# Value projection of a decoder layer: where the second value weights are split and where the second tokens are transposed

## The chip, the cores and the metric

One core of a Trainium2 chip runs the whole layer. The metric is the device time of one execution in microseconds (us). The kernel before took 1835.76 us, the median of three runs (1833.45 to 1837.6).

## What is computed

One layer over 1024 tokens of width 1024, in float32: a half-step SwiGLU network, a token mixer and a second half-step SwiGLU, each followed by a residual sum and a LayerNorm. The part around the change is the input of the token mixer:

```python
x = layer_norm(ALPHA * x + (1 + g1) * (MACARON * y), ln1_g[l], ln1_b[l])
h = modulate(x, sh2, sc2)
y = token_mix(h, w_in[l], b_forget[l], swa_sinks[l], grp_gain[l], w_out[l])
...
proj = h @ w_in
q_a, k_a, v_a, q_b, k_b, v_b, f_logit = jnp.split(proj, idx, axis=-1)
o_a = swa_sink_attention(q_a, k_a, v_a, swa_sinks)
log_f = jax.nn.log_sigmoid(f_logit.astype(jnp.float32) + b_forget.astype(jnp.float32))
o_b = forgetting_attention(q_b, k_b, v_b, log_f)
```

The value projection is the part of `h @ w_in` that gives v_b, v_a and the eight forget logits: 512 + 128 + 8 columns.

## The kernel before, in words

**Precision.** Each float32 operand of a product is held as a high part, rounded to the matrix engine's fp32r format, and a low part, the rest. `split` (lines 101 to 103) makes them: ACT copies the high part (L102), DVE subtracts it (L103). A product is three matmuls, `mm3` (lines 105 to 108: L106, L107, L108).

**Stages.** The first SwiGLU ends with `down` (line 365), which works the tokens in two halves of 512: `xa` are the first tokens, `xb` the second, four tiles of 128 tokens by 1024 each. Its last step multiplies by the gate and subtracts into the tiles of `xb` (L490, L491). The first tokens are normalised and transposed while the second are still being multiplied, with the helper `ln_steps` (line 680). It returns twelve steps: four normalisations of one token tile each, and eight chunks.

- A normalisation (`ln_norm`, line 168) is on DVE two statistics instructions (L158, L159), their merge (L161), an addition (L163), then a power on POOL (L165), then one pass over the tile on DVE (L170).
- A chunk (`ht_chunk`, line 181) transposes one 128-column slice of the four token tiles on PE into a PSUM bank "tp" (L185, four matmuls with the identity), and ACT writes it out with the modulation (L186). `h2_split` (line 699) splits it: the high part on DVE for even chunks (L707), on ACT for odd ones (L705), the low part on DVE (L708).

**The value projection** (lines 733 to 771) multiplies the transposed, modulated tokens by two weights: `wv1`, 320 columns, and `wv2`, 328 columns. `wv_load` brings each in eight slices of 128 rows: one load into a tile of ring "u" (L739, queued on SP), ACT's high copy (L740), DVE's low part (L741). The kernel before calls it for both weights, then runs the four normalisations of the second tokens, then calls `rows2` (line 145), which loads two rows of LayerNorm weights over all partitions (L150) and scales them on ACT (L152).

Then come sixteen projections. The outer loop runs over the halves of the tokens, the next over the two weights, the inner over four token tiles; each projection is eight products, 24 matmuls, into a PSUM bank "mm". ACT copies its high part out (L761), DVE its low part (L762), SP stores both (L763); with the second weight DVE also adds the forget bias (L765). In the first half a projection is followed by at most two of the eight chunks of the second tokens: chunk 1 after projection 2, and so on, chunks 7 and 8 after projection 8. In the second half each is followed by `park_zn` (line 676): an affine of one token tile on DVE (L673, L674) and its store (L678).

After the stage come the projections of queries and keys (`proj`, line 813; their weights are loaded at L528), and then the attention, in which further projections are mixed in.

**What sets the order.** Loads and stores are queued on SP. Buffers are rings: "u" has 6 tiles, "h" 14, "b" 2, "z" and "q" 4 each, "t" 7, "w" 6; PSUM has 3 banks "mm", 2 "tp", 2 "y", 1 "o". A tile is given out again when its last reader is done. The order in which each engine runs its instructions is fixed when the kernel is built, from the program text and from when their operands and buffers are expected.

Of the kernel before, what the change touches and what calls it, by code (L numbers as in the profile page):

```python
# [30 lines left out]
NV1 = 5 * HD  # L31
NV2 = 5 * HD + NH
# [14 lines left out]
def layer_kernel(ctx, tc, xT, x, c, adaT, adab, wg1, wu1, wd1, wqk, wv1, wv2, bf, sinks,  # L47
# [16 lines left out]
    def st(tag, shape, dt=F32):  # L64
        assert 4 * math.prod(shape[1:]) <= RING[tag][1], (tag, shape)
        return mk(sb, shape, dt, tag, RING[tag][0])
# [7 lines left out]
    def psum(tag):  # L74
        return mk(ps, [P, HT], F32, tag, BANK[tag])
# [29 lines left out]
    def mm3(o, lh, ll, rh, rl, start, stop):  # L105
        T.matmul(o, lh, rh, start=start, stop=False)  # L106
        T.matmul(o, lh, rl, start=False, stop=False)  # L107
        T.matmul(o, ll, rh, start=False, stop=stop)  # L108
# [36 lines left out]
    def rows2(i, scale=None, ring="h"):  # L145

        rr = [st("b", [P, D]) for _ in range(2)] if ring == "b" else [st("h", [P, 2, D])]
        rr = rr if ring == "b" else [rr[0][:, q] for q in range(2)]
        for q in range(2):
            DMA.dma_start(rr[q], lnrow[i + q].partition_broadcast(P))  # L150
            if scale is not None:
                A.mul(rr[q], rr[q], scale)  # L152
        return rr
# [510 lines left out]
    def tok(t):  # L664
        return slice(t * P, (t + 1) * P)
# [10 lines left out]
    def park_zn(zt, hf, k, rows, park):  # L676
        affine(zt[k], rows)
        DMA.dma_start(park[tok(hf * 4 + k), :], zt[k])  # L678

    def ln_steps(zt, hf, m, dst, split_to, park=None):  # L680

        def norm(k):
            ln_norm(zt[k])
            if park is not None:
                DMA.dma_start(park[tok(hf * 4 + k), :], zt[k])

        def chunk(d):
            t = dst(d)
            ht_chunk(zt, m, d, t)
            split_to(d, t)  # L690
        return [lambda k=k: norm(k) for k in range(4)] + [lambda d=d: chunk(d) for d in range(KD)]

    def run_all(steps):
        for s in steps:
            s()
# [3 lines left out]
    def h2_split(hf):  # L699
        def f(d, t):  # L700
            if d % 4 == 0:
                h2[hf].append(htiles())
            hi, lo = h2[hf][d // 4]
            if d % 2:
                A.copy(hi[:, d % 4], t)  # L705
            else:
                V.tensor_copy(hi[:, d % 4], t)  # L707
            V.tensor_tensor(lo[:, d % 4], t, hi[:, d % 4].bitcast(F32), ALU.subtract)  # L708
        return f

    def h2c(hf, d):
        hi, lo = h2[hf][d // 4]
        return hi[:, d % 4], lo[:, d % 4]
# [17 lines left out]
    fz = const([P, NT, NH], "fz")  # L731

    def wv_load(src, ncol):
        r = []
        for d0, nk in ((0, 3), (3, 3), (6, 2)):
            w = st("h", [P, 2, nk, ncol], F32R)
            for k in range(nk):
                s = st("u", [P, ncol])
                DMA.dma_start(s, src[:, d0 + k, :])  # L739
                A.copy(w[:, 0, k], s)  # L740
                V.tensor_tensor(w[:, 1, k], s, w[:, 0, k].bitcast(F32), ALU.subtract)  # L741
                r.append((w[:, 0, k], w[:, 1, k]))
        return r

    wva = wv_load(wv1, NV1)
    wvb = wv_load(wv2, NV2)
    steps = ln_steps(xb, 1, mod2, t_tile, h2_split(1))
    run_all(steps[:4])
    r1 = rows2(0, ALPHA, "b")
    for hf in range(2):  # L750
        for pz, (w, ncol) in enumerate(((wva, NV1), (wvb, NV2))):
            for k in range(4):
                t = hf * 4 + k
                p = psum("mm")
                for d in range(KD):
                    hi, lo = h2c(hf, d)
                    mm3(p[:, :ncol], hi[:, k * P:(k + 1) * P], lo[:, k * P:(k + 1) * P],
                        w[d][0], w[d][1], d == 0, d == KD - 1)
                vs = st("w", [P, 5, P], F32R)
                pv = p[:, :5 * HD].rearrange("p (h c) -> p h c", h=5)  # L760
                A.copy(vs[:, :, :HD], pv)  # L761
                V.tensor_tensor(vs[:, :, HD:], pv, vs[:, :, :HD].bitcast(F32), ALU.subtract)  # L762
                DMA.dma_start(vd[pz * 5:pz * 5 + 5, tok(t), :].rearrange("h t c -> t h c"), vs.bitcast(F32))  # L763
                if pz:
                    V.tensor_tensor(fz[:, t], p[:, 5 * HD:NV2], bfb, ALU.add)  # L765
                if hf == 0:
                    if t or pz:
                        steps[3 + t + 4 * pz]()
                    if t == 3 and pz:
                        steps[11]()  # L770
                else:
                    park_zn((xa, xb)[pz], pz, k, r1, xpark[0])

# [432 lines left out]
    def h3_dst(hf):  # L1206
        def f(d):
            if hf == 0:
                hd.append(st("z" if d < 4 else "q", [P, S]))
            return halves(hd[d])[hf]  # L1210
        return f

    def h3_split(hf):
        def f(d, t):
            n = "B%d%d" % (d // 4 + 1, hf + 1)
            if n[2] == "2":
                return
            if d % 4 == 0:
                ops2[n] = htiles()
            split(ops2[n][0][:, d % 4], ops2[n][1][:, d % 4], t)  # L1220
        return f
# [16 lines left out]
    steps = ln_steps(z2[4:], 1, mod3, h3_dst(1), h3_split(1), xpark[1])  # L1238
# [150 lines left out]
```

## Time and profile before

| | |
|---|---|
| median of three runs | 1835.76 us (1833.45 to 1837.6) |
| the profiled execution | 1834.09 us |
| its span, from the first to the last instruction | 1832.1 us |
| mean granted clock of TensorE | 0.985 |
| busy: PE, DVE, ACT | 96%, 84%, 42% of the span |
| sixteen projections of the stage | 661.2 to 731 us |

Shares of the span say which engine is the limit on the whole, not in a stage. In a line of the trace, L12 is line 12 of the kernel; out<-in names the rings, so that `mm<-h,h` at 128x320 or 128x328 is a matmul of the value projection with the first or the second weights. The bracket behind a line tells how long the engine stood idle before it and which instruction ended that. Matmuls overlap, so the distance from one start to the next says more than the duration of one.

### The profile page before, as it was taken

Reading aid. Unit: us, or ns where it says so; the run is one execution under the profiler, and the core shown is the slowest. Engines: PE = TensorE matmul, PEld = TensorE weight load, DVE = VectorE, ACT = ScalarE, POOL = GpSimd, SP = SyncE. Lnnn points to the kernel's source line nnn. Section 1 sums busy time; section 2 is a strip of 40 time slices with the busy share of each in tenths; the row PEclk is TensorE's granted clock in tenths of the full one; section 3 lists DMA queues with packets and bytes.
Section 4 is the critical chain, followed back from the end, with each engine's and each line's share of the span. In section 5 each row is a group of like instructions: output and inputs, shape, how many; then the busy total and the mean of one; then the engine's idle time right before and its main releaser. Section 6 shows DMA issues by size and latency. Waiting matters only on the chain.

```text
span 1832.1 us, 23557 instructions
## 1 busy us (share of the span) xinstructions
PE 1755.3 (96%) x8114; PEld 1444.7 (79%) x8114; DVE 1546.1 (84%) x2805; ACT 764.7 (42%) x1465; POOL 23.0 (1%) x32
## 2 busy tenths in 40 slices
PE   7999999999999989999889899999999999999995
PEld 5788888888888879877667777778888888888884
DVE  7999999999597995378678797899788887878999
ACT  5432333233544442277356461543233333344480
POOL 0000000000000000000000000000000000000000
PEclk9999999999999999999989999999999999999998
DMA  9355555558754245855958863333223232675442
GB/s 360 127 197 178 193 193 193 170 173 290 233 167 143 86 134 180 242 148 154 229 143 198 215 205 107 138 109 128 97 99 131 88 108 92 223 231 166 133 144 80
DMA packets 163175, 303.44 MB, mean 166 GB/s; under 512 B 15384, under 2 KB 47728, under 8 KB 163056
## 3 DMA queue, kind: packets, MB, share of 16 engines
q1 hardware_dynamic: 163056, 301.94, 52.1%
q8 instruction: 64, 1.05, 0.2%
q14 instruction: 55, 0.45, 0.1%
HBM read 224.17 MB, written 77.71 MB: 165 GB/s over the span
## 4 chain that ended last, share of the span: by engine, by line
PE 73%; DVE 15%; DMA 6%; ACT 3%; issue 2%; SPq 0%; POOL 0%; DVEq 0%; ACTq 0%; POOLq 0%
PE y L106 10%; PE y L107 10%; PE y L108 10%; PE mm L106 9%; PE mm L108 9%; PE mm L107 9%; PE o L106 3%; PE o L108 3%; PE o L107 3%; DVE w L103 2%; DVE h L103 2%; DMA q<-cum_d 2%; PE tp L107 1%; PE tp L108 1%; PE tp L1114 1%
## 5 line engine op out<-in xcount | busy, mean ns | idle before, releaser
L102 ACT CAST w<-u 128x512 fp32r<-128x512 f32 x303 | 186.6, 622 | 393.1 <-PE y L108 160.2
L106 PE MATMUL y<-h,w 128*128 128x512 f32 x728 | 287.7, 395 | 5.0 <-ACT h L102 2.1
L107 PE MATMUL y<-h,w 128*128 128x512 f32 x728 | 285.6, 392 | 0.0
L108 PE MATMUL y<-h,w 128*128 128x512 f32 x728 | 285.2, 392 | 0.0
L103 DVE TENSOR_TENSOR w<-u,w 128x512 fp32r<-128x512 f32 x303 | 206.5, 686 | 23.4 <-ACT w L102 22.1
L106 PE MATMUL mm<-h,w 128*128 128x512 f32 x528 | 207.7, 394 | 18.7 <-ACT h L102 15.6
L107 PE MATMUL mm<-h,w 128*128 128x512 f32 x528 | 206.7, 392 | 0.3 <-DVE h L103 0.2
L108 PE MATMUL mm<-h,w 128*128 128x512 f32 x528 | 206.7, 392 | 0.0
L106 PEld LDWEIGHTS y<-h,w 128*128 128x128 f32 x728 | 137.5, 189 | 33.5 <-ACT h L102 2.5
L108 PEld LDWEIGHTS y<-h,w 128*128 128x128 f32 x728 | 137.0, 188 | 26.6
L107 PEld LDWEIGHTS y<-h,w 128*128 128x128 f32 x728 | 137.0, 188 | 26.3
L102 ACT CAST w<-t 128x512 fp32r<-128x512 f32 x106 | 65.5, 621 | 185.1 <-PE mm L108 70.3
L106 PEld LDWEIGHTS mm<-h,w 128*128 128x128 f32 x528 | 100.2, 190 | 40.9 <-ACT h L102 16.0
L107 PEld LDWEIGHTS mm<-h,w 128*128 128x128 f32 x528 | 100.0, 189 | 22.2 <-DVE h L103 1.5
L108 PEld LDWEIGHTS mm<-h,w 128*128 128x128 f32 x528 | 99.9, 189 | 21.3 <-DVE w L103 1.0
L102 ACT CAST z<-u 128x512 fp32r<-128x512 f32 x88 | 54.8, 623 | 105.2 <-PE y L108 46.8
L103 DVE TENSOR_TENSOR z<-u,z 128x512 fp32r<-128x512 f32 x88 | 60.5, 689 | 35.7 <-ACT z L102 35.6
L103 DVE TENSOR_TENSOR t<-tp,t 128x512 fp32r<-128x512 f32 (+1 forms) x126 | 72.8, 586 | 18.4 <-ACT t L102 17.7
L102 ACT CAST t<-tp 128x512 fp32r<-128x512 f32 (+1 forms) x126 | 61.8, 502 | 48.3 <-PE tp L1114 47.4
L102 ACT CAST w<-h 128x512 fp32r<-128x512 f32 x111 | 68.2, 617 | 29.4 <-PE o L108 10.5
L103 DVE TENSOR_TENSOR w<-h,w 128x512 fp32r<-128x512 f32 x111 | 75.6, 686 | 1.8 <-ACT w L102 1.8
L103 DVE TENSOR_TENSOR w<-t,w 128x512 fp32r<-128x512 f32 x106 | 72.8, 689 | 1.4 <-ACT w L102 0.8
(356 smaller groups left out, 3948.1 us busy)
## 6 DMA issues: line engine op xcount, KB each, us to landing
u<-aT SPq DMA_DIRECT2D x154, 256.0 KB, 2.7
q<-in_adaT SPq DMA_DIRECT2D x56, 512.0 KB, 3.4
u<-in_wg SPq DMA_DIRECT2D x92, 256.0 KB, 3.0
u<-in_wu SPq DMA_DIRECT2D x90, 256.0 KB, 2.8
aT<-z SPq DMA_DIRECT2D x44, 512.0 KB, 3.2
h<-in_wd SPq DMA_DIRECT2D x88, 256.0 KB, 4.5
qkd<-w SPq DMA_DIRECT2D x26, 512.0 KB, 4.1
aT<-b SPq DMA_DIRECT2D x22, 512.0 KB, 4.2
```

Of the source, the lines that this page charges most:

```text
L102: A.copy(hi, src)
L103: V.tensor_tensor(lo, src, hi.bitcast(F32), ALU.subtract)
L106: T.matmul(o, lh, rh, start=start, stop=False)
L107: T.matmul(o, lh, rl, start=False, stop=False)
L108: T.matmul(o, ll, rh, start=False, stop=stop)
L1114: T.transpose(pt[:, tok(i - q0)], sps[i][:, tok(j)], ident)
```

## The change

`wv_load` no longer runs its loads and splits. It returns the list that will hold the slices and three functions, which load and split slices 1 to 3, 4 to 6, and 7 and 8. Those of the first weights are run at once. Those of the second weights are put into a list `between`, one behind each of projections 1 to 3; nothing stands behind projection 4; and the eight chunks of the second tokens stand behind projections 5 to 8, two each. The normalisations and the call of `rows2` keep their place. Nothing that is computed changes.

```diff
     def wv_load(src, ncol):
+
         r = []
-        for d0, nk in ((0, 3), (3, 3), (6, 2)):
+
+        def load(d0, nk):
             w = st("h", [P, 2, nk, ncol], F32R)
             for k in range(nk):
                 s = st("u", [P, ncol])
...
                 A.copy(w[:, 0, k], s)
                 V.tensor_tensor(w[:, 1, k], s, w[:, 0, k].bitcast(F32), ALU.subtract)
                 r.append((w[:, 0, k], w[:, 1, k]))
-        return r
-
-    wva = wv_load(wv1, NV1)
-    wvb = wv_load(wv2, NV2)
+        return r, [lambda a=a: load(*a) for a in ((0, 3), (3, 3), (6, 2))]
+
+    wva, load_a = wv_load(wv1, NV1)
+    wvb, load_b = wv_load(wv2, NV2)
+    run_all(load_a)
     steps = ln_steps(xb, 1, mod2, t_tile, h2_split(1))
     run_all(steps[:4])
+    between = [[f] for f in load_b] + [[]] + [steps[4 + 2 * k:6 + 2 * k] for k in range(4)]
     r1 = rows2(0, ALPHA, "b")
...
                 if hf == 0:
-                    if t or pz:
-                        steps[3 + t + 4 * pz]()
-                    if t == 3 and pz:
-                        steps[11]()
+                    run_all(between.pop(0))
                 else:
                     park_zn((xa, xb)[pz], pz, k, r1, xpark[0])
```

## Rows read from the trace of the kernel before

**Rows 1.** The page's parts 1 and 4: busy time, share of the span and instructions of PE; shares of the chain that ended last, by engine.

```profile
PE 1755.3 (96%) x8114; PEld 1444.7 (79%) x8114; DVE 1546.1 (84%) x2805; ACT 764.7 (42%) x1465; POOL 23.0 (1%) x32
...
PE 73%; DVE 15%; DMA 6%; ACT 3%; issue 2%; SPq 0%; POOL 0%; DVEq 0%; ACTq 0%; POOLq 0%
```

**Rows 2.** Windows of the value projection. Columns: the window in us, its length, busy us of PE, PEld, DVE, ACT and POOL, each with its count of instructions, then the granted clock of TensorE, the DMA share and GB/s.

```profile
661.20:671.50 10.30, 10.30 (x72) 10.30 (x70) 9.40 (x22) 4.72 (x10) 0.55 (x1) 1.00 0.61 179
671.50:679.00 7.50, 1.68 (x9) 0.83 (x8) 6.57 (x18) 0.79 (x2) 1.10 (x2) 0.85 0.67 217
679.00:683.50 4.50, 4.50 (x19) 4.42 (x18) 3.42 (x7) 1.43 (x2) 0.55 (x1) 0.50 0.72 218
683.50:705.00 21.50, 21.50 (x153) 21.46 (x152) 17.58 (x28) 9.20 (x16) 0.00 (x0) 1.00 0.50 175
705.00:731.00 26.00, 25.69 (x172) 25.22 (x171) 11.37 (x18) 3.26 (x8) 0.95 (x1) 1.00 0.56 190
```

**Rows 3.** PE in order of time between projections 3 and 5: start us, us from the first start to the last end, engine, line, operation, out<-in, shape, count, and in brackets the idle time before it and what ended it. Equal neighbours are merged (x4).

```profile
672.55 0.30 PE L185 MATMUL tp<-ident,z 128*128 128x128 f32 x1 [0.78 <-DVE z L170]
...
676.30 0.44 PE L185 MATMUL tp<-ident,z 128*128 128x128 f32 x2 [3.20 <-DVE z L170]
678.58 0.69 PE L185 MATMUL tp<-ident,z 128*128 128x128 f32 x2 [1.84 <-DVE z L170]
679.05 0.64 PE L106 MATMUL mm<-h,h 128*128 128x320 f32 x1
...
684.92 0.60 PE L185 MATMUL tp<-ident,z 128*128 128x128 f32 x4
685.28 0.40 PE L106 MATMUL mm<-h,h 128*128 128x328 f32 x1
```

**Rows 4.** DVE in order of time from the first statistics of the second tokens' normalisation to its last step. Columns as in the group above.

```profile
665.44 0.69 DVE L158 BATCH_NORM_STATS2 s_bn<-z 128x6 f32<-128x512 f32 x1
...
668.32 1.88 DVE L741 TENSOR_TENSOR h<-u,h 128x328 fp32r<-128x328 f32 x4 [0.90 <-ACT h L740]
670.12 0.15 DVE L163 TENSOR_SCALAR s_ve<-s_mv 128x1 f32<-128x1 f32 x1
...
670.78 0.90 DVE L741 TENSOR_TENSOR h<-u,h 128x328 fp32r<-128x328 f32 x2
671.59 0.81 DVE L170 TENSOR_SCALAR z<-z,s_mv,s_rs 128x1024 f32<-128x1024 f32 x1
672.32 0.49 DVE L741 TENSOR_TENSOR h<-u,h 128x328 fp32r<-128x328 f32 x1
673.48 0.50 DVE L741 TENSOR_TENSOR h<-u,h 128x328 fp32r<-128x328 f32 x1 [0.67 <-ACT h L740]
...
674.57 0.14 DVE L163 TENSOR_SCALAR s_ve<-s_mv 128x1 f32<-128x1 f32 x1
...
675.44 0.81 DVE L170 TENSOR_SCALAR z<-z,s_mv,s_rs 128x1024 f32<-128x1024 f32 x1
...
678.55 0.44 DVE L762 TENSOR_TENSOR w<-mm,w 128x320 fp32r<-128x320 f32 x1
...
679.78 0.81 DVE L170 TENSOR_SCALAR z<-z,s_mv,s_rs 128x1024 f32<-128x1024 f32 x1 [0.33 <-POOL s_rs L165]
```

**Rows 5.** The chain that ended last, between 661 and 684 us: start us, us, and what it was.

```profile
662.99 4.81 DMA u<-in_wv
...
669.29 3.67 DMA u<-in_wv
...
672.98 0.47 ACT h L740
```

**Rows 6.** DVE in order of time just after the normalisations. Columns as in rows 3.

```profile
680.91 1.22 DVE L673 TENSOR_TENSOR q<-q,b 128x1024 f32<-128x1024 f32 x1
682.88 0.43 DVE L707 CAST h<-t 128x512 fp32r<-128x512 f32 x1 [0.75 <-ACT t L186]
```

**Rows 7.** ACT in order of time, its copies out of PSUM of projections 1 and 3. Columns as in rows 3.

```profile
669.57 0.42 ACT L761 CAST w<-mm 128x320 fp32r<-128x320 f32 x1
...
673.35 0.42 ACT L761 CAST w<-mm 128x320 fp32r<-128x320 f32 x1
```

**Rows 8.** Windows around two gaps of PE in the attention stage. Columns as in rows 2.

```profile
880.00:883.00 3.00, 1.00 (x5) 0.79 (x5) 2.72 (x4) 0.00 (x0) 0.00 (x0) 1.00 1.10 243
1011.00:1016.00 5.00, 2.46 (x10) 1.78 (x9) 5.00 (x13) 1.40 (x5) 1.91 (x1) 0.86 1.02 311
```

**Rows 9.** SP, the engine that issues the loads and stores, in order of time. Columns as in rows 3; the us of a merged row run from the first issue to the last.

```profile
662.55 0.33 SPq L150 DMA_DIRECT2D b<-in_lnrow  x1
662.99 7.01 SPq L739 DMA_DIRECT2D u<-in_wv  x8
670.09 4.24 SPq L528 DMA_DIRECT2D u<-in_wqk  x6
```

**Rows 10.** From the view of line 739, the sixteen loads of both value weights: time from issue to landing.

```profile
DMA to landing us min/median/max: 2.1/2.3/4.3
```

**Rows 11.** Windows after the stage. Columns as in rows 2.

```profile
740.00:783.00 43.00, 43.00 (x207) 35.66 (x207) 13.13 (x33) 13.77 (x33) 0.00 (x0) 1.00 0.78 230
783.00:844.00 61.00, 60.66 (x333) 48.65 (x332) 49.30 (x139) 44.44 (x136) 0.00 (x0) 1.00 0.52 149
```

**Rows 12.** The chain that ended last, in the attention stage: start us, us, and what it was.

```profile
939.12 10.50 DMA q<-cum_d
```

## The prediction

> **What bounds the kernel now.** First the page's engine shares and its chain [rows 1]: PE is busy for 96% of the span and holds 73% of the chain that ended last; DVE comes second with 15%. Time can be won where PE stands still, and the stage to look at is the value projection. I number its projections 1 to 16, eight for the first tokens and eight for the second, each of 24 matmuls. Second, the stage's windows [rows 2]: PE is full from 661.2 to 671.5 us (72 matmuls, projections 1 to 3), works for 1.68 of the next 7.5 us, then runs 4.5 us at a granted clock of 0.50, which is the 1.2 GHz level, and is full at 1.00 from there. Third, PE's order in time [rows 3]: after projection 3 come transposes of the second tokens' first two chunks, two for each token tile, and each pair waits for that tile's normalisation (L170): 0.78, 3.20 and 1.84 us, 5.8 in all. Projection 4 starts at 679.05. It also needs one of the three PSUM banks "mm" back, and the first copy out of one on DVE (L762) starts at 678.55. So both waits are waits for DVE.
>
> Fourth, DVE's order [rows 4], which says why it is late. The normalisations begin at 665.44, but among them stand the eight splits of the second weights (L741, 128x328), and two of these wait for ACT's copy, 0.90 and 0.67 us. Fifth, the chain of waits over this stretch [rows 5]: a load of second weights of 4.81 us, later a last one of 3.67 us and its copy of 0.47, and only then the split and the normalisations of tiles two and three. A transfer that PE does not need before projection 5 holds up what it needs for projection 4.
>
> The order on an engine is not that of the program text: it takes what is ready, earlier text first. In [rows 6] an affine of the second half of the loop (L673, 680.91) runs ahead of a chunk cast of the first half (L707, 682.88) that still waited for ACT. I read the change with that rule.
>
> **The change, part by part.**
>
> The splits leave the normalisations' way. In [rows 4] they take 1.80 us (668.32 to 670.12, four), 0.81 (670.78 to 671.59, two), 0.49 and some 0.4, and the two idles add 0.90 and 0.67: 5.1 us between 665.44 and L762 at 678.55. After the change all eight stand later in the text than the normalisations. I take back 0.2 us, since the first normalisation then waits for POOL with less beside it: from the L163 at 674.57 to its L170 at 675.44 it is 0.87 us, of which one statistics instruction fills some 0.6. **4.9 us earlier** (estimate): L762 at 673.65, projection 4 at 674.15, and PE's gap from 671.6 shrinks to 2.5 us. Bounds: 0, if the list stays as it is, and 7.4 (679.05 − 671.6), if the copy out came before the normalisations; ACT's copy for it (L761) began at 669.57 [rows 7], so that is possible. I take 4.9 because it follows from the order that the rows show.
>
> The transposes move behind projections 5 to 8, two chunks, eight transposes, each. The six that ran inside PE's gap come onto the path. Four in a row from 684.92 let the next matmul start at 685.28 [rows 3], 0.09 us each: **+0.5 us**, or 0 if they still fall into what is left of the gap. The duration of one, 0.30 us at 672.55 [rows 3], is longer than this spacing, since they overlap. The Trainium skill (TensorE: Matmul & The Clock Gate, Part 4: PE-mode transpose) puts one at about 275 ns inside a kernel; the trace agrees with that as a duration, not as a spacing, and by that figure six would cost 1.65 us and the estimated saving in all would be 3.3 us instead of 4.4.
>
> The clock. It fell during the gap; the 15 matmuls and 4 transposes from 679.0 took 4.5 us at 0.50 [rows 2]. At the full clock they take 15 × 0.143 (10.30 us for 72) and 4 × 0.09, 2.5 us: the fall costs 2.0. A gap of 2.5 us remains. Elsewhere a window of 3 us with 2.0 us of gap left the clock at 1.00, and one of 5 us with 2.5 us of gap has 0.86 [rows 8]. The second is nearer: I count the fall as still there, **0 us**; if it does not come, −2.0.
>
> The second weights' loads. They keep their place on SP: the row load (L150) is already ahead of them and the projection weights (L528) behind [rows 9]. They go through a ring of six tiles "u": the first six follow the first weights' splits as now; the last two need the tiles of the first two new splits, now behind the normalisations. The second of these ends by 676.4 (the last normalisation ends at 679.78 + 0.7 − 4.9 = 675.6, then two splits of 0.4). A load of 3.67, a copy of 0.47 and a split of 0.50 put the eighth slice at 681.1 [rows 4, 5]. PE asks for it after projection 4 (24 × 0.143, to 677.6), 0.5 of transposes and 21 matmuls, 3.0 us: also 681.1. **0 us**, and up to 0.6 if the load takes the longest landing, 4.3 us [rows 10]. What hides the load is projections 4 and 5; without them the whole 4.6 us of load, copy and split would show. Queued behind a late load on SP are the value stores (L763) and L528's weights, which nobody wants before 731.
>
> DVE and ACT in projections 5 to 8. 3.6 us of splits move into a stretch where DVE works 17.58 of 21.5 us, and the affines, which stand late in the text, can slide to 705 to 731, where it works 11.37 of 26 [rows 2]. ACT works less than half of either. **0 us.** The last two chunks stand behind projection 8 before and after, so what projection 9 waits for is the same work as now.
>
> After the stage PE is full to 783 and for 60.66 of 61 us to 844 [rows 11], so a start 4.4 us earlier is an end 4.4 us earlier, unless something later does not move with PE.
>
> Sum: −4.9 + 0.5 + 0 = **−4.4 us** against the profiled execution's 1834.09 us (span 1832.1): 1829.7. The median of the three runs, 1835.76, is 1.7 above that execution, and the runs spread over 4 us. A measurement here can tell about 0.2%, 3.7 us, from no change, and the forecast lies just beyond that.
>
> **The rivals.**
>
> Same side, the clock stays up through the shorter gap: −4.4 − 2.0 = −6.4, 1827.7. For it: the gap of 2.0 us in [rows 8]. Against: the one of 2.5 us.
>
> No change, because the edit does not do what it says: the list goes by readiness [rows 6], and whenever the normalisations wait for POOL a split or its idle may slip in again. Against: each wait has the next tile's statistics to fill it. With all eight back in place the time is 1834.1.
>
> No change, because the gain is swallowed: later PE waits for transfers, a broadcast load of 10.50 us at 939.12 [rows 12]. If the start of that load hung on something other than work behind PE, the 4.4 us would end there: 1834.1. Against: it needs buffers that PE's earlier work releases.
>
> Slower: the second weights come late for projection 5. Place: the first two new splits, which release the "u" tiles for loads seven and eight. If affines stand ahead of them on DVE, at 1.22 us each [rows 6], eight cost 9.8 us: the eighth slice comes at 690.9, PE waits 9.8 us, and a second fall of the clock costs 2.0: −4.4 + 9.8 + 2.0 = +7.4, 1841.5. With that fall counted, two affines ahead eat the gain. For it: affines do run early [rows 6]. Against: a split is earlier in the text, and ACT, done with the last L761 at 673.8 [rows 7], has its copy ready.
>
> Either side: the lists of later stages are laid differently. No row prices it; I bound it by half of the longest load wait above, 5 us.
>
> **How the numbers follow.** Forecast 0.34; clock stays 0.24; edit without effect 0.08; swallowed 0.18; weights late 0.10; later lists 0.06. Faster by over 0.2% (3.7 us): 0.28 of the forecast, 0.23 of the second case and 0.03 of the last: 0.54. Slower: 0.10, 0.03 of the last and 0.02 of the swallowed: 0.15. The same: 0.31. Range: down to the whole gap gone with the clock up, −7.4 + 0.5 − 2.0 = −8.9, 1825.2, and a little lower for the spread, 1824.5; up to no change at the highest of the runs, 1837.5. Left out are the late weights and the far ends of the rest.
>
> **What would show it.** Right: no 328-wide L741 between the first L158 and the last L170; the first L762 near 673.7; a gap of PE before projection 4 near 2.5 us; L185 behind the first 328-wide matmuls; the stage's last matmul, at 731 before, 4 to 6 us earlier. Wrong: PE waiting for L741 in projection 5, affines ahead of the new splits, or a stage that ends earlier while the span does not.

## The result

The changed kernel takes 1826.35 us, the median of four runs (1823.94 to 1827.29), against 1834.62 for the kernel before in the same runs: a ratio of 0.995, 95% interval 0.9933 to 0.9968. Six runs more on another occasion gave 1824.66 us against 1832.05, 0.9958 (0.9944 to 0.9972). Both medians lie lower there; the ratio is the same within its interval. That is 7 to 9 us, where 4.4 were forecast.

The value projection accounts for it. I measure the stage from the first statistics instruction on DVE (L158), which starts at 665.44 us before and 665.45 after, to the first matmul of the query and key projections: 66.28 us before, 58.92 after, **7.4 us less**. The end of the stage before the change, on PE; the same row after it stands in the next section:

```profile
731.72 0.50 PE L106 MATMUL y<-h,w 128*128 128x512 f32 x1 [1.03 <-ACT w L102]
```

### The profile page after: what moved, and what is told of

It is laid out like the page before. It is cut to its first block, busy times and chain, and to the rows that moved or that the text cites. A ratio compares the mean times of both kernels' runs of the same rounds, so it can differ in the third digit from the quotient of the medians.

```text
span 1825.4 us, 23553 instructions
## 1 busy us (share of the span) xinstructions
PE 1752.3 (96%) x8114; PEld 1442.8 (79%) x8114; DVE 1544.9 (85%) x2805; ACT 763.6 (42%) x1465; POOL 22.5 (1%) x32
## 4 chain that ended last, share of the span: by engine, by line
PE 79%; DVE 10%; DMA 5%; ACT 3%; issue 2%; SPq 1%; POOL 0%; DVEq 0%; ACTq 0%; POOLq 0%
PE y L106 10%; PE y L107 10%; PE y L108 10%; PE mm L106 9%; PE mm L108 9%; PE mm L107 9%; PE o L106 3%; PE o L107 3%; PE o L108 3%; PE tp L107 2%; PE tp L108 2%; PE tp L106 2%; PE tp L1115 1%; DVE h L103 1%; DMA q<-cum_d 1%
```

## The profile after

The changed file is two to four lines longer in this stretch, so L739, L740, L741 are now L741, L742, L743, and L761, L762, L763 are L765, L766, L767. Most of the kernels of the experiments have one line more, and there the copy out on DVE is L767.

Windows of the stage after the change; they answer to [rows 2], columns as there.

```profile
661.20:671.50 10.30, 10.30 (x72) 10.29 (x71) 10.04 (x23) 4.12 (x9) 1.10 (x2) 1.00 0.48 152
671.50:673.00 1.50, 0.97 (x7) 0.58 (x6) 1.49 (x5) 0.43 (x1) 0.27 (x1) 1.00 0.00 0
673.00:683.50 10.50, 10.08 (x67) 9.81 (x68) 9.74 (x21) 3.53 (x7) 0.96 (x2) 1.00 0.76 219
683.50:705.00 21.50, 21.50 (x153) 21.45 (x152) 21.50 (x32) 8.36 (x15) 0.00 (x0) 1.00 0.73 259
705.00:724.00 19.00, 18.33 (x124) 18.06 (x122) 4.85 (x11) 2.76 (x7) 0.95 (x1) 1.00 0.61 196
```

Where PE worked for 1.68 of 7.5 us and then 4.5 us at the 1.2 GHz level, it now loses about a microsecond, and the granted clock is 1.00 throughout. DVE is full from 683.5 to 705, and PE does not notice. It is not the splits that fill it, whose last runs at 678.69 (two in a row), but affines: 13 affine instructions (L673, L674) run in this stretch instead of 9, and 2 instead of 6 are left for the rest of the stage.

PE in order of time; answers to [rows 3].

```profile
671.76 0.70 PE L185 MATMUL tp<-ident,z 128*128 128x128 f32 x4
673.04 0.42 PE L106 MATMUL mm<-h,h 128*128 128x320 f32 x1 [0.58 <-DVE w L766]
...
677.20 0.42 PE L106 MATMUL mm<-h,h 128*128 128x328 f32 x1 [0.38 <-DVE w L766]
...
680.89 0.60 PE L185 MATMUL tp<-ident,z 128*128 128x128 f32 x4
...
724.37 0.50 PE L106 MATMUL y<-h,w 128*128 128x512 f32 x1 [1.03 <-ACT w L102]
```

Projection 4 starts at 673.04 instead of 679.05. Four transposes still run in its small gap, of the first two token tiles, whose normalisations are done; the chunks' other two tiles follow at 680.89. What PE waits for is now named plainly: a copy out of a bank on DVE, 0.58 us before projection 4 and 0.38 before projection 5.

DVE in order of time; answers to [rows 4].

```profile
665.45 0.69 DVE L158 BATCH_NORM_STATS2 s_bn<-z 128x6 f32<-128x512 f32 x1
...
668.78 0.81 DVE L170 TENSOR_SCALAR z<-z,s_mv,s_rs 128x1024 f32<-128x1024 f32 x1
...
672.51 0.48 DVE L766 TENSOR_TENSOR w<-mm,w 128x320 fp32r<-128x320 f32 x1
673.32 0.81 DVE L170 TENSOR_SCALAR z<-z,s_mv,s_rs 128x1024 f32<-128x1024 f32 x1 [0.33 <-POOL s_rs L165]
674.05 0.20 DVE L161 BATCH_NORM_AGGREGATE s_mv<-s_bn 128x2 f32<-128x12 f32 x1
674.17 0.45 DVE L743 TENSOR_TENSOR h<-u,h 128x328 fp32r<-128x328 f32 x1
...
675.53 0.81 DVE L170 TENSOR_SCALAR z<-z,s_mv,s_rs 128x1024 f32<-128x1024 f32 x1 [0.44 <-POOL s_rs L165]
676.25 0.49 DVE L743 TENSOR_TENSOR h<-u,h 128x328 fp32r<-128x328 f32 x1
676.67 0.48 DVE L766 TENSOR_TENSOR w<-mm,w 128x320 fp32r<-128x320 f32 x1
```

No split stands in front of the first three normalisations. The first copy out runs at 672.51, inside the third normalisation's wait for POOL. The second stands behind three splits at 676.67, though ACT had done its part at 670.2 us (its copy starts at 669.73 and takes 0.42): projection 5 pays for that. DVE even stood idle for 0.44 us ahead of the L170 at 675.53 while this copy out was ready. The Trainium skill (TensorE: Matmul & The Clock Gate, Part 1, under the heading on the array's architecture) calls DVE's queue strictly first in, first out; the trace agrees, by that idle of 0.44 us.

The last two loads of second weights, on SP, and the first copy on ACT that waited for them:

```profile
674.64 0.80 SPq L741 DMA_DIRECT2D u<-in_wv  x2
```

```profile
676.93 0.47 ACT L742 CAST h<-u 128x328 fp32r<-128x328 f32 x1 [4.54 <-DMA u<-in_wv]
```

They are issued 5.4 us later than the last one before (669.29) and land in time.

## The experiments

Theory A: the gain comes from DVE's list. Without the splits among the normalisations, the first copy out of a bank comes early, projection 4 starts early, and the clock has no time to fall. Rival B: it comes from the chunks' new place on PE. Rival C: it is the normalisations themselves, not the bank, that PE waited for. Stage times are measured as above, so that the start of the stage in each execution, which varies by up to 1.4 us, is out.

**Splits alone moved.**

```diff
-    between = [[f] for f in load_b] + [[]] + [steps[4 + 2 * k:6 + 2 * k] for k in range(4)]
+    chunks = [[], steps[4:5], steps[5:6], steps[6:7], steps[7:8], steps[8:9], steps[9:10], steps[10:12]]
+    between = [load_b[k:k + 1] + chunks[k] for k in range(8)]
```

> Only the second weights' splits move behind projections 1 to 3; the chunks stay where they were (one behind each projection from the second). Theory A, the gain is DVE's list (the first copy out of a bank comes early): the first copy out starts near 672.5 us, the first matmul of the query projections near 724.4 to 725.5 us (731.72 before, 724.37 with the change), the time 6 to 8 us under the kernel before. Rival B, the gain is the chunks' new place on PE: the stage ends near 731 and the time is that of before within 2 us.

Measured: 1825.95 us against 1832.17, ratio 0.9966 (0.9956 to 0.9977). Here is the first copy out, on DVE, and then the first matmul after the stage, on PE:

```profile
672.08 0.48 DVE L767 TENSOR_TENSOR w<-mm,w 128x320 fp32r<-128x320 f32 x1
```

```profile
724.17 0.50 PE L106 MATMUL y<-h,w 128*128 128x512 f32 x1 [1.03 <-ACT w L102]
```

The stage takes 59.14 us. This half of the change alone gives 7.1 of the 7.4 us.

**Chunks alone moved.**

```diff
     run_all(load_a)
+    run_all(load_b)
...
-    between = [[f] for f in load_b] + [[]] + [steps[4 + 2 * k:6 + 2 * k] for k in range(4)]
+    between = [[]] * 4 + [steps[4 + 2 * k:6 + 2 * k] for k in range(4)]
```

> Only the chunks move behind projections 5 to 8; the second weights are split ahead of the normalisations as before. Theory A: the first copy out stays near 678 to 679 us, the gap of PE and the fall of the clock stay, the stage ends within 1 us of 731.7 and the time is that of before within 2 us. Rival B: the stage ends 4 us or more earlier and the time falls by as much.

Measured: 1832.52 us against 1832.17, ratio 1.0 (0.9989 to 1.0011); the stage takes 66.18 us. PE in order of time:

```profile
672.30 0.41 PE L185 MATMUL tp<-ident,z 128*128 128x128 f32 x2 [0.37 <-DVE z L170]
...
675.88 0.44 PE L185 MATMUL tp<-ident,z 128*128 128x128 f32 x2 [3.17 <-DVE z L170]
678.15 0.69 PE L185 MATMUL tp<-ident,z 128*128 128x128 f32 x2 [1.83 <-DVE z L170]
```

The same waits as in [rows 3], although the two chunks now stand behind projection 5 in the text and no longer behind projections 2 and 3: PE had nothing else that was ready, so they were put into the gap again. Rival B falls.

**Splits behind the normalisations, but ahead of the projections.**

```diff
     run_all(steps[:4])
-    between = [[f] for f in load_b] + [[]] + [steps[4 + 2 * k:6 + 2 * k] for k in range(4)]
+    run_all(load_b)
+    between = [[], steps[4:5], steps[5:6], steps[6:7], steps[7:8], steps[8:9], steps[9:10], steps[10:12]]
```

> The chunks stay at their old places; all eight splits of the second weights stand right behind the normalisations and ahead of the projections. Theory A says that PE waits for the bank, not for the normalisations: the normalisations come as early as with the change (the last near 675.5 us), but the first copy out stands behind seven splits, two of which need late loads, so near 678 to 680 us; PE's gap stays and the time is within 3 us of before. Rival C, the normalisations are what PE waits for: the stage ends near 726 us and the time is 5 us or more under before.

Measured: 1832.87 us against 1832.17, ratio 1.0004 (0.999 to 1.0017); the stage takes 64.91 us. DVE in order of time, the last normalisation and the first two copies out:

```profile
675.32 0.81 DVE L170 TENSOR_SCALAR z<-z,s_mv,s_rs 128x1024 f32<-128x1024 f32 x1 [0.44 <-POOL s_rs L165]
676.05 1.72 DVE L743 TENSOR_TENSOR h<-u,h 128x328 fp32r<-128x328 f32 x4
677.69 0.88 DVE L767 TENSOR_TENSOR w<-mm,w 128x320 fp32r<-128x320 f32 x2
```

The normalisations are as early as with the change (675.53 there), yet 6.0 of the 7.4 us are not won: the copy out waits behind seven splits. None of these waits for a load; DVE's only idles ahead of the copy out are two of 0.44 us for POOL. Rival C falls. PE in order of time has eight more transposes, of the next two chunks, ahead of projection 4:

```profile
677.53 1.97 PE L185 MATMUL tp<-ident,z 128*128 128x128 f32 x8 [0.66 <-ACT t L186]
679.15 0.61 PE L106 MATMUL mm<-h,h 128*128 128x320 f32 x1
```

The first copy out ends near 678.1, so the last microsecond before projection 4 is theirs and not the bank's. The waits of [rows 3] name the normalisations because the transposes stood next on PE; the bank was the later lock.

**The clock by itself.** The kernel before, with matmuls that nobody reads in PE's gap:

```diff
...
+                if t == 2 and not pz:
+                    dm = psum("y")
+                    for d in range(KD):
+                        hi, lo = h2c(0, d)
+                        mm3(dm[:, :ncol], hi[:, :P], lo[:, :P], w[d][0], w[d][1], d == 0, d == KD - 1)
                 vs = st("w", [P, 5, P], F32R)
```

> The kernel before with 24 more matmuls behind projection 3 into a bank that nobody reads, so that PE works in its gap. DVE's waits are those of before. If the fall of the clock costs 2.0 us as the sum has it, the granted clock stays at 1.00 through 683 us, projection 4 starts where it did (679 us) and the stage ends 1.5 to 2.5 us earlier, near 729.7 us. If the fall costs nothing by itself, or the added matmuls get in the way, the stage ends at 731.7 us or later.

Measured: 1830.31 us against 1832.17, ratio 0.9991 (0.9977 to 1.0004): not separable from no change by time. Its windows:

```profile
671.50:679.00 7.50, 6.06 (x40) 5.26 (x39) 6.91 (x18) 0.89 (x2) 1.65 (x3) 1.00 0.58 191
679.00:683.50 4.50, 4.48 (x32) 4.21 (x32) 4.50 (x7) 3.27 (x5) 0.00 (x0) 1.00 0.74 225
```

The clock stays at 1.00. Its first copy out on DVE and the end of its stage on PE:

```profile
677.50 0.44 DVE L767 TENSOR_TENSOR w<-mm,w 128x320 fp32r<-128x320 f32 x1
```

```profile
728.88 0.50 PE L106 MATMUL y<-h,w 128*128 128x512 f32 x1 [1.03 <-ACT w L102]
```

From the first copy out to the stage's end it is 51.4 us against 53.2 before (678.55 to 731.72), and projection 4 starts 0.5 us behind the copy out in both: **1.8 us** is the fall's price, where the sum had 2.0. The stage ended earlier than expected because the copy out, too, came 1 us earlier in this execution.

**The change once more.** No edit.

> The changed kernel itself once more, beside the three below and timed in more rounds, with a second profile. The value projection's end comes within 0.5 us of 724.4 us again (first matmul of the query projections); if the differences of 1 to 2 us that arise in the attention stage are those of single executions, this profile's span differs from 1825.4 us by up to 2 us without a difference in the stage. Against the kernel before: 6 to 8 us less.

Measured: 0.9958, as given above; the stage takes 58.92 us again. But three of the output's last stores (columns: line, engine, operation, tile, count, shortest, median and longest ns, first and last start in us) come at different times in the two executions. The kernel before, the change, the change again:

```profile
L1323 SPq DMA_DIRECT2D out<-z x3: 332/332/333, 1821.4 to 1826.0; - x3
```

```profile
L1324 SPq DMA_DIRECT2D out<-z x3: 332/332/333, 1814.7 to 1819.2; - x3
```

```profile
L1324 SPq DMA_DIRECT2D out<-z x3: 332/332/333, 1812.8 to 1817.3; - x3
```

The first is 6.7 us ahead of before at the end, the second 8.6, with one and the same stage time. Of the 1.9 us between them 0.5 arises ahead of the stage (the second one's first L158 starts at 664.96); the rest arises in the attention stage, and there the granted clock falls at different places in the two, though the program is the same. The same window in the first and in the second:

```profile
874.00:880.00 6.00, 4.51 (x13) 3.75 (x14) 6.00 (x8) 0.21 (x1) 0.00 (x0) 0.72 0.81 245
```

```profile
874.00:880.00 6.00, 5.88 (x26) 4.94 (x27) 6.00 (x9) 2.31 (x4) 0.00 (x0) 1.00 0.84 257
```

From 1106 to 1114 us it is the other way round, 1.00 and 0.79. Single executions gain or lose up to some 3 us after the stage: that with the clock kept was 2.8 us ahead of before at the stage's end and 0.3 behind at the stores. So the stage's time is what tells these kernels apart, and the ratio needs many runs.

**Splits one projection later.**

```diff
-    between = [[f] for f in load_b] + [[]] + [steps[4 + 2 * k:6 + 2 * k] for k in range(4)]
+    between = [[]] + [[f] for f in load_b] + [steps[4 + 2 * k:6 + 2 * k] for k in range(4)]
```

> The changed kernel with the second weights' splits one projection later each (behind projections 2, 3 and 4). With the change projection 5 waited 0.38 us for the second copy out, which stood on DVE behind three splits. Theory A: the first two copies out now stand ahead of the splits, projection 5's wait for a bank goes; the last slices come up to 1 us later, near 680.5 us, about when they are asked for; the stage ends within 1 us of 724.4 us. Rival, late weights: PE waits 2 us or more for a split in projection 5 and the stage ends at 726 us or later.

Measured: 1826.55 us against 1832.05, ratio 0.9972 (0.996 to 0.9984); the stage takes 59.40 us, 0.5 more than with the change. The wait for the second bank is gone, but the last split waits 0.40 us for its copy, and PE is busy for 4.88 of the 5 us from 679 and for 15.81 of the 16 from 684, where the change has both full. No gain on the change.

**Normalisations spread.** The third and fourth stand behind projections 1 and 2, the splits behind 2, 3 and 4.

```diff
-    run_all(steps[:4])
+    run_all(steps[:2])
-    between = [[f] for f in load_b] + [[]] + [steps[4 + 2 * k:6 + 2 * k] for k in range(4)]
+    between = [steps[2:3], steps[3:4] + load_b[:1], load_b[1:2], load_b[2:3]] + [steps[4 + 2 * k:6 + 2 * k] for k in range(4)]
```

> The changed kernel with the third and fourth normalisations behind projections 1 and 2 and the splits behind projections 2, 3 and 4. Theory A: the first copy out of a bank now stands ahead of half of the statistics, near 668 us, so projection 4 follows projection 3 without a gap; what is left of the loss (0.6 us before projection 4, 0.4 before projection 5 and two half-empty stretches) goes, and the stage ends 1 to 2 us earlier than with the change, near 723 us. Rival: PE then waits for the last splits or normalisations instead and the stage ends at 724.4 us or later.

Measured: 1824.8 us against 1832.05, ratio 0.9959 (0.9943 to 0.9974); the stage takes 58.48 us, 0.4 less than with the change and not the 1 to 2 expected. The first copy out is at 668.30 and the gap before projection 4 is gone, but PE in order of time shows what came in its place:

```profile
678.24 0.42 PE L107 MATMUL mm<-h,h 128*128 128x328 f32 x1 [0.74 <-DVE h L743]
```

Projection 5, reached earlier, waits for a split. The last normalisation (L170 at 676.57) comes 0.8 us later in the stage than with the change, and PE does not wait for it: the reverse of the test of rival C, with the same answer. Time cannot tell this version from the change.

**Splits last.** All three groups behind projection 4, so that the second weights come late.

```diff
-    between = [[f] for f in load_b] + [[]] + [steps[4 + 2 * k:6 + 2 * k] for k in range(4)]
+    between = [[], [], [], load_b] + [steps[4 + 2 * k:6 + 2 * k] for k in range(4)]
```

> The changed kernel with all eight splits of the second weights behind projection 4: the late weights on purpose. Theory A, that an engine takes what is ready: the splits are ready long before and still run from about 676 us, when the normalisations are done, with at most an affine or two between; the last slice comes near 681.5 us, PE waits 1 to 2.5 us in projection 5, and the stage ends near 726 us, still 5 us ahead of before. Rival, late weights as the prediction priced them: affines go first, PE waits 5 us or more, and the time is that of before or above.

Measured: 1824.65 us against 1832.05, ratio 0.9961 (0.9945 to 0.9976); the stage takes 58.92 us, as with the change. DVE in order of time, with one affine among the splits, as theory A has it, and then PE's wait:

```profile
678.28 0.49 DVE L743 TENSOR_TENSOR h<-u,h 128x328 fp32r<-128x328 f32 x1
678.68 1.22 DVE L673 TENSOR_TENSOR q<-q,b 128x1024 f32<-128x1024 f32 x1
679.82 0.90 DVE L743 TENSOR_TENSOR h<-u,h 128x328 fp32r<-128x328 f32 x2
```

```profile
679.63 0.42 PE L106 MATMUL mm<-h,h 128*128 128x328 f32 x1 [0.23 <-ACT h L742]
```

PE loses a few tenths here and saves the 0.38 us at the second bank. My 1 to 2.5 us were too much, the rival's 5 far off. In the places tried, all of them behind the normalisations and the first copy out in the text, it hardly matters where the splits stand: the stage takes 58.48 to 59.40 us.

**A gap of the forecast's size.** The first copy out done twice, then three times, so that PE's gap is longer and all else is the change.

```diff
-                V.tensor_tensor(vs[:, :, HD:], pv, vs[:, :, :HD].bitcast(F32), ALU.subtract)
+                for _ in range(2 if t == 0 and not pz else 1):
+                    V.tensor_tensor(vs[:, :, HD:], pv, vs[:, :, :HD].bitcast(F32), ALU.subtract)
```

> The changed kernel with the first copy out of a bank done twice on DVE (the same result written again), so that its bank comes free one place later, near 674.6 us, and PE's gap before projection 4 becomes the 2.5 us of the prediction (four transposes in it). Forecast's branch: the granted clock falls near 676 us and costs up to 2.0 us, projection 4 starts near 674.7 and the query projections near 727.5 us (724.4 with the change, plus 1.6 for the bank, plus 1.5 to 2 for the clock). Rival branch: the clock stays at 1.00 and they start near 725.7 us.

> As the kernel before it, with the first copy out done three times: its bank comes free near 676.7 us, behind the last normalisation, and PE's gap is some 4.5 us with eight transposes in it. Both branches expect the clock to fall, as it did in the gap of the kernel before. Projection 4 starts near 676.8 us; with a fall of 1.8 to 2.0 us the query projections start near 729.5 us, without one near 727.7 us.

One execution each: 1825.5 and 1828.65 us, beside 1833.59 for the kernel before. Windows of the gap and of what follows, done twice, and then done three times:

```profile
672.20:674.70 2.50, 0.71 (x5) 0.23 (x3) 2.17 (x8) 0.19 (x1) 0.55 (x1) 1.00 0.00 0
674.70:684.00 9.30, 9.24 (x63) 9.27 (x64) 8.86 (x16) 3.19 (x7) 0.67 (x1) 1.00 0.84 251
```

```profile
671.80:676.00 4.20, 0.72 (x6) 0.25 (x4) 3.42 (x10) 0.17 (x1) 1.22 (x2) 1.00 0.07 10
676.00:680.00 4.00, 4.00 (x17) 3.83 (x18) 4.00 (x11) 2.70 (x5) 0.00 (x0) 0.57 0.76 228
680.00:684.00 4.00, 4.00 (x29) 4.00 (x28) 2.87 (x5) 0.52 (x2) 0.00 (x0) 1.00 1.03 313
```

In the gap that I had forecast, the clock stays up, and the stage takes 59.84 us, 6.4 less than before: the figure of the first rival. In the gap of 4.2 us it falls as it did in the kernel before, and the stage takes 63.14. These are single executions, and two executions of one program were seen above to differ in where the clock falls, so they do not show that a gap of 2.5 us always keeps it.

Done twice, the second copy out, on DVE, stands where the prediction had the first, right behind the third normalisation, and here is the start of projection 4 on PE:

```profile
674.17 0.44 DVE L767 TENSOR_TENSOR w<-mm,w 128x320 fp32r<-128x320 f32 x1
```

```profile
674.76 0.38 PE L106 MATMUL mm<-h,h 128*128 128x320 f32 x1
```

From that place projection 4 comes 4.3 us earlier than before, and 1.7 us later than with the change.

## Why the prediction was right, and where it was short

The mechanism was right; the size came out as in the first rival (clock up, 0.24), not as in the forecast (0.34). The two main errors, 1.1 us on the bank and 1.8 us on the clock, point the same way, so both medians lie near the lower end of the range. Of the signs of being right the L185 behind the first 328-wide matmuls came; the others missed in size or failed: the first copy out came 1.2 us ahead of its 673.7, the wait before projection 4 was 0.6 us and not 2.5, two splits stood ahead of the last L170, and the stage ended 7.4 us earlier, not 4 to 6. None of the three signs of being wrong came.

**What bounds the stage.** Right. The splits of the second weights and their late loads stood among the normalisations on DVE and, through these, ahead of the first copy out of a bank. Moving them alone gives 7.1 of 7.4 us; moving the chunks alone gives 0.1.

**The step "4.9 us earlier".** Right in kind, short in size: projection 4 starts 6.0 us earlier. I took the 5.1 us of splits and idles out of the list of [rows 4] and left the rest in its order, with the copy out behind the third normalisation. But without the splits the statistics of all four tiles run ahead, and by 672.5 none are left to fill the third one's wait for POOL (672.46 to 673.32). The copy out, the next thing ready, goes in there. By the reading rule of [rows 6] I should have laid the list out anew. The kernel with the copy out done twice parts the two: at the place that I had assumed the gain is 4.3 us, not 4.9, since the third normalisation waits for POOL with no statistics beside it, and the new place adds 1.7. Two splits likewise slipped into the fourth one's wait, ahead of the last L170.

**The transposes, +0.5 us.** Four of the six still run in the gap, so the term is 0.2. By the 275 ns of the Trainium skill (TensorE: Matmul & The Clock Gate, Part 4: PE-mode transpose), given there for bf16, the two left would cost an estimated 0.55 us and the sum below would be −6.9, further from what the stage shows.

**The clock, 0 us.** Wrong branch. The fall costs 1.8 us when taken alone (2.0 in the sum), and it does not come: not in the 0.6 us wait that is left, and not in the one execution with a gap of 2.5 us. The row of 2.5 us in 1011 to 1016 [rows 8] had seemed nearer; but there PE stands idle for 2.54 us without a break, and in the gap of 2.5 us for 1.73 at most, between transposes. By the longest idle the row of 880 to 883, 2.0 us in one piece, was the nearer one. The kernel with a gap of 4.2 us fits neither row: the clock falls, though its longest idle is 1.76. What decides is open.

Three rows of PE after its longest idle: the two gaps of [rows 8] in the kernel before, then the gap of 2.5 us (copy out done twice):

```profile
882.17 0.45 PE L1089 MATMUL mm<-z,z 128*128 128x384 f32 x1 [2.00 <-DVE s_mneg L1092]
...
1014.53 0.60 PE L1119 MATMUL o<-t,h 128*128 128x384 f32 x1 [2.54 <-DVE t L103]
```

```profile
674.19 0.44 PE L185 MATMUL tp<-ident,z 128*128 128x128 f32 x2 [1.73 <-DVE z L170]
```

**The second weights' loads, 0 us.** Right about the loads: issued at 674.64, copied at 676.93. I had missed that the second copy out now stands behind three splits: 0.38 us in projection 5. DVE and ACT in projections 5 to 8, 0 us: right, though not for my reason. The splits were done by 679.5 and the affines came earlier, not later; DVE was full and PE did not wait.

With these sizes the sum is −6.0 − 1.8 + 0.2 + 0.4 = −7.2, against 7.4 measured in the stage.

**The gain reaches the end.** Right on the whole: 7.4 us at the stage's end, 6.7 and 8.6 at the last stores of two executions. The rival that it would be swallowed by a transfer in the attention stage fell; that stage adds scatter, not a limit. The scatter goes with falls of the clock at different places; what makes them differ was not tried.

**Late weights**, the slower rival: its place is real (PE waits for a split or a copy with the normalisations spread and with the splits last), its price is not. The affines hardly go ahead, since the splits are ready and stand earlier in the text.

## What to carry to other kernels

When a wait is named after one operand, look for the second lock behind it: here PE waited in name for a normalisation, and the bank's copy out, later on the same engine's list, decided. Work on an in-order engine that is not needed yet belongs behind the work that another engine waits for, in the text too, whether it waits for a transfer or not: of the 5.1 us taken out here 3.5 were the splits themselves and 1.6 their waits, and seven splits that waited for no load kept 6.0 of the 7.4 us from being won. In the places tried, how far behind hardly mattered. And when instructions are taken out of such a list, lay the whole list out again by what is ready, rather than shift the old one.

## What the runs showed of the hardware that was not expected

A gap of PE of 2.5 us, with six transposes in and around it, left the granted clock at 1.00, while one of 4.2 us with eight lowered it to the 1.2 GHz level from 676 to near 679.4 us (one execution each), and the kernel before lost 1.8 us by a fall in its gap of 7.5. Two executions of one program, with the same stage time to 0.01 us, ended 1.9 us apart, and in the attention stage the clock fell at different places in them.
